# Modulation products queued behind named VectorE instructions, and gate scaling on ScalarE, in a one-core prefix network

## The chip, the cores and the metric

The kernel runs on one core of one Trainium2 chip. The metric is the device time of one execution in microseconds (us), given as the median of several runs.

## The reference, cut to what matters

A prefix network of two layers works on 256 latent tokens and 256 context tokens (together T = 512) of width 1024. Layer 0 is a hybrid mixer (HGRN2 scans in both directions over four heads of 128, and attention over eight heads of 64) and a convolutional FFN; layer 1 is an SSD mixer and an FFN. Both norms of every layer are modulated by vectors that come from the condition, one set for the latent and one for the context stream:

```python
for l in range(DEPTH):
    sh_m, sc_m, g_m, sh_f, sc_f, g_f = jnp.split(s_lat @ w_mod[l] + b_mod[l], 6, axis=-1)
    csh_m, csc_m, cg_m, csh_f, csc_f, cg_f = jnp.split(s_ctx @ w_mod[l] + b_mod[l], 6, axis=-1)
    u = modulate(h, norm_mix[l], sh_m, sc_m)       # rms_norm(h) * (1 + sc) + sh
    ...
    h = h + g_m[:, None] * y
    h = h + g_f[:, None] * conv_ffn(modulate(h, norm_ffn[l], sh_f, sc_f), ...)
```

The HGRN forget gates are `lb + (1 - lb) * sigmoid(f)`, and the keys `(1 - lb) * sigmoid(-f)`. The product of the condition with `w_mod` does not depend on the tokens, so it can be made at any time before its chunk (0 to 5, in the order of the split) is used.

## The kernel before

Activations are kept as fp32 split into a high and a low part (xhi, xlo; mhi, mlo; hh, hl). A weight tile of 128x1024 is loaded as `raw`, rounded by ScalarE into `whi` (L135) and the rest taken by VectorE into `wlo` (L137), and each product is three TensorE matmuls (L144): xlo by whi, xhi by whi, xhi by wlo. A step of 512 columns is about 0.23 us. Four buffers each hold raw, whi and wlo.

Layer 0's mixer goes: the first norm, with seven projections made along with it (L735 to L743); two HGRN pairs (`hgrn_pair`, two heads each); attention (`attention`: value projection L637, then `heads` and `mix` for four pairs of heads); the output projection (L774 to L782); then the FFN's norm and the FFN. In `hgrn_pair` a ladder of eight levels (L524 to L577) runs: at each level small matmuls of K by Q, then VectorE multiplications of Q, K and the running products f (L520). Then come K by Q in 128x128 (L584), four scalings for each head (`scl`, L589), transposes of K (L602), the states (L608), attention by v (L615), the states by Q (L619), and for each head y = ps * gain * gate (L625), its sum of squares by a matmul with ones (L628) and the scaled y (L630). Projections of the next stage are what TensorE does between these small matmuls. In `mix` each of the 32 softmax rows of tiles is: scores on TensorE, a bias for the latent stream (L691), a maximum (L693), the exponential on ScalarE (L695), a reciprocal and a scaling (L697) on VectorE, transposes back on TensorE (L700), and after four of them the product with v (L706).

A part of the modulation is made on VectorE. A unit is one 128x1024 tile `wv` of w_mod, multiplied with the two condition rows and summed: two instructions on `junk` (L270), here called halves, each with a read of the accumulator. Eight units make one chunk of modT (L276). At most three units are loaded ahead (`vec_fetch`). 64 units are made in this way: chunks (layer 0) 3, 4 and 2 in the mixer, and five more (chunk 5 of layer 0, and 0, 1, 3, 4 of layer 1) in FFN 0.

The instructions' order on each engine comes from a scheduler that works through the program in priority order as operands come free; each engine then runs its list strictly in order. `vec(n)` (L259) makes n units, and `issue_after(self.last_mm.ins)` keeps a unit in the list behind the most recent projection matmul. It is called after projections (L491, L506, L638, L650) and, for what is left, before the output projection (L771); FFN 0 calls it too. `after(...)` holds an instruction behind given ones.

The gate scalings of HGRN are VectorE instructions (L501, L503), eight of each, and the diagonal 32x32 blocks of the HGRN matrix are copied by VectorE (L552), four for each pair.

## Time and profile before

| | us |
|---|---|
| runs of the kernel before | 1226.21, 1227.2, 1228.07 (median 1227.2) |
| the profiled execution | 1228.9, its span 1227.1 |
| TensorE busy | 1196.0 (97%), mean granted clock 0.998 |
| VectorE busy | 923.7 (75%) |
| ScalarE busy | 593.1 (48%) |

The program's stages in the span are: first norm and first seven projections to about 71 us; HGRN pair 0 with its ladder to 138; pair 1 with its ladder to 212; attention to 327; output projection to 356; the FFN's norm to 363; FFN 0 after that. A window view gives for each stretch the busy time of every engine; where TensorE's falls short of the stretch, or its granted clock short of 1.00, time was lost. The timeline gives the instruction that began late and, in brackets, how long its engine had been idle and what ended that.

### The profile page before, as it was taken

How to read it: one execution, taken by the hardware profiler on the slowest of the kernel's cores; microseconds unless marked ns; L12 is line 12 of the kernel's file. 1: busy time of each engine (PE TensorE's matmuls, PEld its weight loads, DVE VectorE, ACT ScalarE, POOL GpSimd, SP SyncE). 2: the span in 40 equal slices, each digit the busy share in tenths (PEclk: the TensorE clock that was granted, in tenths of full speed). 3: DMA queues.
4: the chain of work that ended last, by engine and by line, in shares of the span. 5: the costliest groups of instructions: out<-in, count | busy, mean ns of one | idle time of the engine just before them, and what ended most of it. 6: DMA issues, size and time to landing. Idle time of an engine off the chain costs nothing.

```text
span 1227.1 us, 19142 instructions
## 1 busy us (share of the span) xinstructions
PE 1196.0 (97%) x7519; PEld 979.6 (80%) x7519; DVE 923.7 (75%) x1596; ACT 593.1 (48%) x923; POOL 0.2 (0%) x4
## 2 busy tenths in 40 slices
PE   5999999999999999999999999999999999999998
PEld 3687787766678888888888887778778798999998
DVE  4799999688669999984344458598989786766665
ACT  4554545798545331333133336647363644645452
POOL 0000000000000000000000000000000000000000
PEclk9999999999999999999999999999999999999999
DMA  9852635413064677752332234444344244665663
GB/s 379 316 178 71 222 106 169 136 60 125 27 213 148 207 213 227 226 178 82 104 102 83 90 119 139 154 138 160 113 138 138 86 148 144 190 187 184 181 185 106
DMA packets 55097, 189.35 MB, mean 154 GB/s; under 512 B 7136, under 2 KB 10848, under 8 KB 53728
## 3 DMA queue, kind: packets, MB, share of 16 engines
q1 hardware_dynamic: 51984, 185.17, 47.1%
q10 hardware_dynamic: 3024, 2.97, 0.8%
q8 instruction: 59, 0.97, 0.3%
q14 instruction: 30, 0.25, 0.1%
HBM read 187.00 MB, written 1.11 MB: 153 GB/s over the span
## 4 chain that ended last, share of the span: by engine, by line
PE 82%; DVE 8%; issue 2%; ACT 2%; DMA 1%; ACTq 0%; DVEq 0%
PE a L144 49%; PE s L144 17%; PE b L706 1%; PE s L161 1%; PE s L162 1%; PE s L163 1%; DVE junk L270 1%; DVE Q L520 1%; PE b L972 1%; PE b L999 1%; PE b L1004 1%; DVE wlo L137 1%; DVE K L520 1%; PE b L700 1%; PE b L937 1%
## 5 line engine op out<-in xcount | busy, mean ns | idle before, releaser
L135 ACT CAST whi<-raw 128x1024 fp32r<-128x1024 f32 (+1 forms) x234 | 240.9, 1032 | 342.7 <-PE a L144 275.2
L137 DVE TENSOR_TENSOR wlo<-raw,whi 128x1024 fp32r<-128x1024 f32 (+1 forms) x234 | 280.4, 1199 | 101.5 <-ACT whi L135 99.9
L144 PE MATMUL a<-xhi,wlo 128*128 128x512 f32 (+1 forms) x740 | 268.7, 370 | 3.6 <-ACT va L640 1.9
L144 PE MATMUL a<-xhi,whi 128*128 128x512 f32 (+1 forms) x740 | 271.4, 367 | 0.0
L144 PE MATMUL a<-xlo,whi 128*128 128x512 f32 (+1 forms) x740 | 258.5, 367 | 3.0 <-DVE xlo L378 3.0
L144 PEld LDWEIGHTS a<-xhi,wlo 128*128 128x128 f32 x740 | 139.0, 188 | 31.1 <-issue 4.1
L144 PEld LDWEIGHTS a<-xlo,whi 128*128 128x128 f32 x740 | 137.4, 188 | 31.8 <-issue 4.6
L144 PEld LDWEIGHTS a<-xhi,whi 128*128 128x128 f32 x740 | 139.4, 188 | 25.5 <-issue 3.6
L270 DVE SCALAR_TENSOR_TENSOR junk<-wv,rows 128x1024 f32<-128x1024 f32 x128 | 156.3, 1221 | 1.9
L144 PE MATMUL s<-xhi,wlo 128*128 128x512 f32 (+1 forms) x376 | 128.5, 342 | 0.0
L144 PE MATMUL s<-xhi,whi 128*128 128x512 f32 (+1 forms) x376 | 128.2, 341 | 0.0
L144 PE MATMUL s<-xlo,whi 128*128 128x512 f32 (+1 forms) x376 | 121.6, 341 | 0.4 <-ACT pr L695 0.4
L144 PE MATMUL a<-hh,whi 128*128 128x256 f32 (+1 forms) x359 | 120.1, 335 | 0.0
L144 PE MATMUL a<-hh,wlo 128*128 128x256 f32 (+1 forms) x359 | 113.2, 335 | 0.0
L144 PE MATMUL a<-hl,whi 128*128 128x256 f32 (+1 forms) x359 | 112.6, 336 | 0.0
L391 DVE SCALAR_TENSOR_TENSOR h<-a,modT,h 128x256 f32<-128x256 f32 x90 | 40.8, 481 | 69.4 <-PE a L144 69.2
L144 PEld LDWEIGHTS s<-xhi,wlo 128*128 128x128 f32 x376 | 70.6, 188 | 9.5 <-issue 0.4
L144 PEld LDWEIGHTS s<-xhi,whi 128*128 128x128 f32 x376 | 70.5, 188 | 9.1
L144 PEld LDWEIGHTS s<-xlo,whi 128*128 128x128 f32 x376 | 69.2, 188 | 10.2 <-ACT pr L695 0.8
L144 PEld LDWEIGHTS a<-hh,whi 128*128 128x128 f32 x359 | 67.6, 188 | 7.8
L144 PEld LDWEIGHTS a<-hl,whi 128*128 128x128 f32 x359 | 65.7, 188 | 8.2 <-DVE hl L399 0.5
L144 PEld LDWEIGHTS a<-hh,wlo 128*128 128x128 f32 x359 | 65.9, 188 | 7.8
(340 smaller groups left out, 1794.1 us busy)
## 6 DMA issues: line engine op xcount, KB each, us to landing
raw<-in_wup SPq DMA_DIRECT2D x88, 512.0 KB, 4.1
wv<-in_wmodT SPq DMA_DIRECT2D x64, 512.0 KB, 4.4
raw<-in_win SPq DMA_DIRECT2D x41, 512.0 KB, 3.7
raw<-in_wdn SPq DMA_DIRECT2D x32, 448.0 KB, 3.3
raw<-in_wo SPq DMA_DIRECT2D x24, 512.0 KB, 3.6
wm<-in_wmod SPq DMA_DIRECT2D x8, 1024.0 KB, 11.0
wv<-in_wmod SPq DMA_DIRECT2D x16, 512.0 KB, 4.6
raw<-in_wdn SPq DMA_DIRECT2D x16, 512.0 KB, 3.6
```

Of the source, the lines that this page charges most:

```text
L135: nc.scalar.copy(hi, raw)
L137: nc.vector.tensor_tensor(out=lo, in0=raw, in1=hi.bitcast(F32), op=ALU.subtract)
L144: self.last_mm = self.nc.tensor.matmul(ps, w, x, start=(first and i == 0), stop=(last and i == 2))
L161: mm(ps, xhi[:, k, tok], wlo[:, kk, :], start=(k == 0), stop=False)
L162: mm(ps, xhi[:, k, tok], whi[:, kk, :], start=False, stop=False)
L163: mm(ps, xlo[:, k, tok], whi[:, kk, :], start=False, stop=(k == NK - 1))
L270: nc.vector.scalar_tensor_tensor(out=self.junk, in0=w, scalar=1.0, in1=self.rows[:, s], op0=ALU.mult, op1=ALU.mult, accum_out=self.dots[:, ...
L391: self.nc.vector.scalar_tensor_tensor(out=self.h[:, n, s * S:(s + 1) * S], in0=ps[:, off:off + S], scalar=self.mod(l, chunk, n, s), in1=se ...
L520: mul = lambda o, t: nc.vector.tensor_tensor(out=o, in0=o, in1=t, op=ALU.mult)
L700: nc.tensor.transpose(pt[:, b * P:(b + 1) * P], pr[:, b * P:(b + 1) * P], self.ident)
L706: nc.tensor.matmul(po[64 * e:64 * e + 64, :S], va[:, b, hd * 64:(hd + 1) * 64], pTs[e][:, b, :], start=(b == 0), stop=(b == nkey - 1))
L937: nc.tensor.transpose(pt[:, b * P:(b + 1) * P], dst[:, b * P:(b + 1) * P], self.ident)
```

## The change

- A unit is issued as two separate halves. `half(x)` issues the next one, held behind the instruction x, or behind nothing if none is named.
- The wait for the last projection matmul is gone. Four halves stand behind the last xlo of the first norm (after each of four projections of pair 0: the one projection that is not made with the norm); one behind the Q, K, f multiplications of each level of the HGRN ladder (eight in a pair), four behind the last `scl`, one behind the scaling of each softmax row of tiles with qt == 1 (16), and two after each of the output columns 1 to 4, behind the sum of squares (`self.summed`).
- The units left over before the output projection are no longer made there; FFN 0 makes the rest, its halves held behind nothing.
- The chunks of layer 0 are made in the order 2, 4, 3 in place of 3, 4, 2.
- The gate scalings become ScalarE activations (Identity with scale and bias; Copy with scale), and the diagonal copies ScalarE copies.

```diff
-            with self.tc.issue_after(self.last_mm.ins):
-                for s in STREAMS:
-                    nc.vector.scalar_tensor_tensor(out=self.junk, in0=w, scalar=1.0, in1=self.rows[:, s], op0=ALU.mult,
-                                                   op1=ALU.mult, accum_out=self.dots[:, k, s:s + 1])
-            self.vec_fetch()
...
+    def half(self, after=None):
+        if not self.half_done:
+            if not self.fetched:
+                return
+            w, l, c, k = self.half_done = self.fetched.pop(0)
...
+            s = 0
+        else:
+            (w, l, c, k), self.half_done, s = self.half_done, None, 1
+        with self.after((after,) if after else ()):
+            nc.vector.scalar_tensor_tensor(out=self.junk, in0=w, scalar=1.0, in1=self.rows[:, s], op0=ALU.mult,
+                                           op1=ALU.mult, accum_out=self.dots[:, k, s:s + 1])
+        if s == 0:
+            return
+        self.vec_fetch()
...
-                        self.vec_queue([(0, 3), (0, 4), (0, 2)])
+                        self.vec_queue([(0, 2), (0, 4), (0, 3)])
...
-                    self.vec()
+                    if pr == 0:
+                        for _ in range(4):
+                            self.half(self.low.ins)
...
-                    nc.vector.tensor_scalar(out=ff, in0=ff, scalar1=om[:, d, hd:hd + 1], scalar2=lb[:, d, hd:hd + 1],
-                                            op0=ALU.mult, op1=ALU.add)
-                    nc.vector.tensor_scalar(out=kk, in0=kk, scalar1=om[:, d, hd:hd + 1], scalar2=None, op0=ALU.mult)
+                    nc.scalar.activation(ff, ff, AF.Identity, scale=om[:, d, hd:hd + 1], bias=lb[:, d, hd:hd + 1])
+                    nc.scalar.activation(kk, kk, AF.Copy, scale=om[:, d, hd:hd + 1])
...
-                    nc.vector.tensor_copy(blocks(j, 32, j, 32), attc[j:j + 32].rearrange("p (a b) t -> p a b t", a=4))
+                    nc.scalar.copy(blocks(j, 32, j, 32), attc[j:j + 32].rearrange("p (a b) t -> p a b t", a=4))
...
             for a in range(2):
-                mul(one(a, m, 0), one(a, m, 1))
+                x = mul(one(a, m, 0), one(a, m, 1))
+            self.half(x.ins)
...
-            scl(K[:, 1, hh, P:2 * P], tf(0, 0))
+            x = scl(K[:, 1, hh, P:2 * P], tf(0, 0))
+        for _ in range(4):
+            self.half(x.ins)
...
-                        nc.vector.tensor_scalar(out=pr, in0=pr, scalar1=sm[:, 2:3], scalar2=None, op0=ALU.mult)
+                        x = nc.vector.tensor_scalar(out=pr, in0=pr, scalar1=sm[:, 2:3], scalar2=None, op0=ALU.mult)
+                        if qt == 1:
+                            self.half(x.ins)
...
-            self.vec(NK * 3)
...
                     self.residual(0, 2, n, ps, part, True)
+                if 0 < n < 5:
+                    self.half(self.summed.ins)
+                    self.half(self.summed.ins)
```

The calls `self.vec(2)`, `self.vec(3)` and `self.vec()` after the value projections and the head projections go too. Lines of the changed kernel are 8 to 14 further down from there on.

How the lists move is shown at three places. The first is VectorE in the first norm. `junk` is a half, `mrow`, `mres`, `modT` and `A` make a late piece of chunk 1's modulation, `nt` is the normed activation, and `xlo` its low part for the last tiles. Before:

```order
L201 TENSOR_REDUCE mres_456<-m_399 128x2x4
L464 TENSOR_TENSOR lbm<-lbo,lbx 128x8
L270 SCALAR_TENSOR_TENSOR junk,dots_660<-wv_625,rows 128x1024
L210 TENSOR_TENSOR modT<-mres_456,c_bmod 128x2x4
L465 RECIPROCAL lbm<-lbm 128x8
L213 SCALAR_TENSOR_TENSOR A<-modT,c_gains 128x4
L270 SCALAR_TENSOR_TENSOR junk,dots_660<-wv_625,rows 128x1024
L375 SCALAR_TENSOR_TENSOR nt_494<-h,A,fr_173 128x256 x2
L375 SCALAR_TENSOR_TENSOR nt_528<-h,A,fr_173 128x256
L378 SCALAR_TENSOR_TENSOR xlo<-nt_494,modT,xhi 128x256 x2
L378 SCALAR_TENSOR_TENSOR xlo<-nt_528,modT,xhi 128x256
L375 SCALAR_TENSOR_TENSOR nt_528<-h,A,fr_173 128x256
```

After the change:

```order
L201 TENSOR_REDUCE mres_456<-m_399 128x2x4
L210 TENSOR_TENSOR modT<-mres_456,c_bmod 128x2x4
L213 SCALAR_TENSOR_TENSOR A<-modT,c_gains 128x4
L385 SCALAR_TENSOR_TENSOR nt_494<-h,A,fr_173 128x256 x2
L385 SCALAR_TENSOR_TENSOR nt_528<-h,A,fr_173 128x256
L388 SCALAR_TENSOR_TENSOR xlo<-nt_494,modT,xhi 128x256 x2
L388 SCALAR_TENSOR_TENSOR xlo<-nt_528,modT,xhi 128x256
L385 SCALAR_TENSOR_TENSOR nt_528<-h,A,fr_173 128x256
L137 TENSOR_TENSOR wlo_633<-raw_630,whi_632 128x1024
L388 SCALAR_TENSOR_TENSOR xlo<-nt_528,modT,xhi 128x256
L278 SCALAR_TENSOR_TENSOR junk,dots_660<-wv_623,rows 128x1024 x2
L769 CAST masks<-mf 128x160
```

The halves that stood among and ahead of nt and xlo now stand behind the last xlo.

The second is TensorE at the end of HGRN pair 1 (K transposed, states b<-v,kT, b<-att,v, b<-Q,Sx, sums b<-sq,ones); L161 to L163 are matmuls of attention's value projection, and L144 (a<-xhi,wlo) the first head projection. Before:

```order
L619 MATMUL b_1996<-Q_1195,Sx_1973 128x256 x2
L161 MATMUL a_2034<-wlo_2131,xhi 128x512
L162 MATMUL a_2034<-whi_2130,xhi 128x512
L163 MATMUL a_2034<-whi_2130,xlo 128x512
L161 MATMUL a_2035<-wlo_2131,xhi 128x512
L628 MATMUL b_2007<-sq_2003,ones 128x512
L615 MATMUL b_2012<-att_1625,v_1198 128x256 x4
L619 MATMUL b_2012<-Q_1195,Sx_1973 128x256 x2
L162 MATMUL a_2035<-whi_2130,xhi 128x512
L163 MATMUL a_2035<-whi_2130,xlo 128x512
L161 MATMUL a_2036<-wlo_2131,xhi 128x512
L162 MATMUL a_2036<-whi_2130,xhi 128x512
```

After the change:

```order
L616 MATMUL b_1989<-c_ident,K_1217 128x128 x4
L629 MATMUL b_2000<-att_1604,v_1219 128x256 x2
L622 MATMUL b_1978<-v_1219,kT_1976 128x128 x4
L629 MATMUL b_2000<-att_1604,v_1219 128x256 x2
L633 MATMUL b_2000<-Q_1216,Sx_1977 128x256 x2
L642 MATMUL b_2011<-sq_2007,ones 128x512
L629 MATMUL b_2016<-att_1604,v_1219 128x256 x4
L633 MATMUL b_2016<-Q_1216,Sx_1977 128x256 x2
L642 MATMUL b_2026<-sq_2023,ones 128x512
L144 MATMUL a_2170<-xhi,wlo_2174 128x512
L144 MATMUL a_2170<-xhi,whi_2173 128x512
```

The value projection's matmuls that stood between the small ones now stand further ahead, among the ladder's levels, and none is left here.

The third is VectorE at the start of the output projection; `h` is the residual of one output column, `nacc` the running sum of squares, wlo the weight split of a later column, which TensorE needs for column 4 (s_3361 before, s_3366 after the change). Before:

```order
L399 TENSOR_TENSOR mlo<-b_3182,mhi 128x256
L391 SCALAR_TENSOR_TENSOR h<-a_3218,modT,h 128x256 x2
L391 SCALAR_TENSOR_TENSOR h<-a_3253,modT,h 128x256 x2
L391 SCALAR_TENSOR_TENSOR h<-a_3289,modT,h 128x256 x2
L137 TENSOR_TENSOR wlo_3358<-raw_3355,whi_3357 128x1024
L318 TENSOR_TENSOR nacc_3245<-nacc_3245,nsq_3280 128x512
L391 SCALAR_TENSOR_TENSOR h<-s_3325,modT,h 128x256 x2
L318 TENSOR_TENSOR nacc_3245<-nacc_3245,nsq_3316 128x512
L137 TENSOR_TENSOR wlo_3395<-raw_3392,whi_3394 128x1024
L318 TENSOR_TENSOR nacc_3245<-nacc_3245,nsq_3352 128x512
L137 TENSOR_TENSOR wlo_3431<-raw_3428,whi_3430 128x1024
L137 TENSOR_TENSOR wlo_3467<-raw_3464,whi_3466 128x1024
```

After the change:

```order
L401 SCALAR_TENSOR_TENSOR h<-a_3284,modT,h 128x256 x2
L401 SCALAR_TENSOR_TENSOR h<-s_3325,modT,h 128x256
L328 TENSOR_TENSOR nacc_3236<-nacc_3236,nsq_3271 128x512
L278 SCALAR_TENSOR_TENSOR junk,dots_2649<-wv_3017,rows 128x1024
L401 SCALAR_TENSOR_TENSOR h<-s_3325,modT,h 128x256
L278 SCALAR_TENSOR_TENSOR junk,dots_2649<-wv_3017,rows 128x1024
L328 TENSOR_TENSOR nacc_3236<-nacc_3236,nsq_3311 128x512
L278 SCALAR_TENSOR_TENSOR junk,dots_2649<-wv_3088,rows 128x1024
L328 TENSOR_TENSOR nacc_3236<-nacc_3236,nsq_3352 128x512
L278 SCALAR_TENSOR_TENSOR junk,dots_2649<-wv_3088,rows 128x1024
L137 TENSOR_TENSOR wlo_3363<-raw_3360,whi_3362 128x1024
L286 TENSOR_TENSOR modT<-dots_2649,c_bmod 128x16
```

Four halves now stand ahead of that wlo. Ten more follow up to the last `nacc` of the norm: four that are held behind `nacc`, and six that FFN 0's calls make.

## Rows read from the trace of the kernel before

**Rows 1.** The page: span, and busy time of each engine.
```profile
span 1227.1 us, 19142 instructions
...
PE 1196.0 (97%) x7519; PEld 979.6 (80%) x7519; DVE 923.7 (75%) x1596; ACT 593.1 (48%) x923; POOL 0.2 (0%) x4
```

**Rows 2.** Windows by stage: length, busy time of PE, PEld, DVE, ACT, POOL, clock, DMA.
```profile
71.00:122.00 51.00, 49.16 (x720) 40.83 (x718) 50.62 (x97) 26.47 (x44) 0.00 (x0) 1.00 0.37 124
...
138.00:205.00 67.00, 66.04 (x794) 54.10 (x793) 66.30 (x122) 29.56 (x46) 0.00 (x0) 1.00 0.48 151
205.00:212.00 7.00, 5.06 (x22) 3.51 (x21) 6.77 (x13) 4.58 (x9) 0.00 (x0) 1.00 0.57 166
...
363.00:600.00 237.00, 237.00 (x1017) 190.44 (x1017) 196.62 (x311) 79.67 (x102) 0.00 (x0) 1.00 0.59 183
```

**Rows 3.** Windows of line L270 (the halves) alone: length, DVE busy, clock, DMA.
```profile
219.00:363.00 144.00, 1.23 (x2) 1.00 0.31 98
363.00:545.00 182.00, 90.93 (x148) 1.00 0.67 209
```

**Rows 4.** Groups of DVE by form: count, busy us, mean ns, idle before.
```profile
L137 DVE TENSOR_TENSOR wlo<-raw,whi 128x1024 fp32r<-128x1024 f32 x194 | 236.8, 1222 | 78.6 <-ACT whi L135 77.0
L270 DVE SCALAR_TENSOR_TENSOR junk<-wv,rows 128x1024 f32<-128x1024 f32 x128 | 156.3, 1221 | 1.9
...
L552 DVE COPY att<-attc 32x256 f32<-32x256 f32 x8 | 2.3, 283 | 0.1
```

**Rows 5.** Timeline of DVE in the first norm: start, us, instruction.
```profile
53.18 1.22 DVE L270 SCALAR_TENSOR_TENSOR junk<-wv,rows 128x1024 f32<-128x1024 f32 x1
...
57.48 1.22 DVE L270 SCALAR_TENSOR_TENSOR junk<-wv,rows 128x1024 f32<-128x1024 f32 x1
...
59.81 1.27 DVE L378 SCALAR_TENSOR_TENSOR xlo<-nt,modT,xhi 128x256 fp32r<-128x256 f32 x3
```

**Rows 6.** Timeline of PE in the first norm; in brackets idle before and releaser.
```profile
59.05 0.40 PE L144 MATMUL b<-xhi,wlo 128*128 128x512 f32 x1
60.74 0.50 PE L144 MATMUL a<-xlo,whi 128*128 128x512 f32 x1 [1.30 <-DVE xlo L378]
```

**Rows 7.** Waits of PE: us in total, times, longest.
```profile
PE a L144 <- ACT va L640: 1.9, 1, 1.9
...
PE b L542 <- DVE Q L520: 1.0, 1, 1.0
...
PE m L199 <- DVE mrow L193: 0.9, 1, 0.9
```

**Rows 8.** Timeline of DVE in pair 1: last ladder scaling, first y.
```profile
195.56 0.47 DVE L589 TENSOR_SCALAR K<-K,f 128x128 f32<-128x128 f32 x2
...
203.30 0.75 DVE L625 SCALAR_TENSOR_TENSOR h<-b,c_small,h 128x512 f32<-128x512 f32 x1
```

**Rows 9.** Timeline of PE in pair 1: first level, end of the tail, head projection.
```profile
166.25 0.76 PE L542 MATMUL b<-h,kc 128*32 128x32 f32 x64
...
208.21 0.80 PE L163 MATMUL a<-whi,xlo 128*128 128x512 f32 x1
...
209.31 0.39 PE L163 MATMUL s<-whi,xlo 128*128 128x512 f32 x1
211.64 0.50 PE L144 MATMUL a<-xhi,wlo 128*128 128x512 f32 x1 [1.94 <-ACT va L640]
```

**Rows 10.** Windows: softmax part of attention, output, the slowed stretch, its gap; a dense part.
```profile
239.25:323.60 84.35, 82.73 (x409) 56.20 (x407) 67.81 (x158) 71.20 (x162) 0.00 (x0) 1.00 0.24 77
327.42:358.13 30.71, 30.70 (x174) 25.49 (x177) 19.78 (x33) 14.66 (x19) 0.00 (x0) 1.00 0.40 123
212.30:215.70 3.40, 3.40 (x10) 2.62 (x9) 3.33 (x5) 2.03 (x3) 0.00 (x0) 0.51 0.91 266
...
266.00:303.00 37.00, 36.14 (x173) 24.06 (x171) 32.84 (x71) 34.22 (x74) 0.00 (x0) 1.00 0.32 109
```

**Rows 11.** Timeline of ACT before pair 1, and a window of ACT alone there.
```profile
138.78 1.28 ACT L499 ACT_TABLE_LOAD   x1
140.07 0.60 ACT L499 ACTIVATE f<-a 128x512 f32<-128x512 f32 x1
...
131.30:166.20 34.90, 16.85 (x24) 1.00 0.63 196
```

More of the change, by code (lines that the diff above doesn't have):

```diff
@@ L259, in vec @@
     def vec(self, n=1):
+        for _ in range(2 * n):
+            self.half()
+    def half(self, after=None):
         nc = self.nc
-        for _ in range(n):
+        if not self.half_done:
             if not self.fetched:
                 return
-            w, l, c, k = self.fetched.pop(0)
+            w, l, c, k = self.half_done = self.fetched.pop(0)
             if k == 0:
                 self.dots = self.w.tile([P, NK, 2], F32, tag="dots", bufs=2, name=self.nm("dots"))
-            with self.tc.issue_after(self.last_mm.ins):
-                for s in STREAMS:
-                    nc.vector.scalar_tensor_tensor(out=self.junk, in0=w, scalar=1.0, in1=self.rows[:, s], op0=ALU.mult,
-                                                   op1=ALU.mult, accum_out=self.dots[:, k, s:s + 1])
-            self.vec_fetch()
-            if k < NK - 1:
-                continue
-            dst = self.modT[:, l, 8 * c:8 * c + 8, :]
-            nc.vector.tensor_tensor(out=dst, in0=self.dots, op=ALU.add,
-                                    in1=cust(self.bmod[:, l, 8 * c:8 * c + 1], 0, [[1, 8], [0, 2]]))
-            if c in (1, 4):
-                which = (c - 1) // 3
-                nc.vector.scalar_tensor_tensor(
-                    out=self.A[:, l, which], in0=dst, scalar=1.0, op0=ALU.add, op1=ALU.mult,
-                    in1=cust(self.gains[:, 2 * which + l, 0:1], 0, [[1, NK], [0, 2]]))
@@ L284, in mod @@
+        nc.vector.tensor_tensor(out=dst, in0=self.dots, op=ALU.add,
+                                in1=cust(self.bmod[:, l, 8 * c:8 * c + 1], 0, [[1, 8], [0, 2]]))
+        if c in (1, 4):
+            which = (c - 1) // 3
+            nc.vector.scalar_tensor_tensor(
+                out=self.A[:, l, which], in0=dst, scalar=1.0, op0=ALU.add, op1=ALU.mult,
+                in1=cust(self.gains[:, 2 * which + l, 0:1], 0, [[1, NK], [0, 2]]))
     def mod(self, l, chunk, k, s):
@@ L317, in sumsq @@
             self.act_set(6, last)
-        nc.vector.tensor_tensor(out=self.acc[:, tok], in0=self.acc[:, tok], in1=sq, op=ALU.add)
+        self.summed = nc.vector.tensor_tensor(out=self.acc[:, tok], in0=self.acc[:, tok], in1=sq, op=ALU.add)
     def norm_r(self, ps, t0, n, meanwhile):
@@ L377, in norm_u @@
             u = nc.scalar.activation(xhi[:, k, tok], t[:, rel], AF.Identity, bias=sh)
-            nc.vector.scalar_tensor_tensor(out=xlo[:, k, tok], in0=t[:, rel], scalar=sh, in1=xhi[:, k, tok].bitcast(F32),
-                                           op0=ALU.add, op1=ALU.subtract)
+            self.low = nc.vector.scalar_tensor_tensor(out=xlo[:, k, tok], in0=t[:, rel], scalar=sh, op0=ALU.add,
+                                                      in1=xhi[:, k, tok].bitcast(F32), op1=ALU.subtract)
         return u
@@ L545, in hgrn_pair @@
                     for a in range(2):
-                        nc.vector.tensor_tensor(out=flat(Q, a), in0=q.rearrange("p h t -> p (h t)"), in1=flat(f, a),
-                                                op=ALU.mult)
+                        x = nc.vector.tensor_tensor(out=flat(Q, a), in0=q.rearrange("p h t -> p (h t)"), in1=flat(f, a),
+                                                    op=ALU.mult)
+                    self.half(x.ins)
                     continue
@@ L696, in mix @@
                         nc.vector.reciprocal(sm[:, 2:3], sm[:, 1:2])
-                        nc.vector.tensor_scalar(out=pr, in0=pr, scalar1=sm[:, 2:3], scalar2=None, op0=ALU.mult)
+                        x = nc.vector.tensor_scalar(out=pr, in0=pr, scalar1=sm[:, 2:3], scalar2=None, op0=ALU.mult)
+                        if qt == 1:
+                            self.half(x.ins)
                         pt = self.ps_b()[:, :w]
```

7 lines of the change are left out of this document (3 added, 4 removed).

## The prediction

> **What bounds the kernel now.** I read the page first: TensorE is busy for 1196.0 of 1227.1 us, VectorE for 75%, ScalarE for 48% [rows 1]. So a change to VectorE's list can win only what TensorE loses now, about 31 us in all, and only the part of it that lies in the first 363 us, where the halves are moved. The window view by stage shows how little that is [rows 2]: TensorE idles for 1.84 us of 71 to 122, for 0.96 of 138 to 205, for 1.94 of 205 to 212, and for nothing in FFN 0. In the same rows VectorE is full in HGRN (50.62 of 51, 66.30 of 67), so the halves there do stand in TensorE's way a little. The windows of the halves' line show the other side [rows 3]: between 219 and 363 us there is one half, and 74 of the 128 lie in FFN 0, where TensorE is never short. The change carries 20 halves out of HGRN, where VectorE is full, and ten out of FFN 0, and puts them into attention (16) and the output projection (14), where there are none. What counts is whether those two stages have room on VectorE.
>
> **Price of a half.** 1221 ns, and a wlo 1222 ns [rows 4]; with overlaps a step is 1.15 to 1.2 us, and I take 1.2.
>
> **First norm: -2.2.** Four halves sit among nt and xlo [rows 5], and TensorE, which had started a matmul of 0.23 us at 59.05, gets its next xlo at 60.74, a gap of 1.46 us that ends at VectorE's xlo [rows 6]. The wait of 0.9 on mrow [rows 7] has a half ahead of mrow as well. The lists show the halves behind the last xlo, so both go, about 1.4 and 0.8. The next thing that could be late is the weight split, which the matmuls need anyway; I leave a tenth or two for it.
>
> **Ladder of pair 0: -0.8 (0 to -1.9).** TensorE's idle time here is 1.84 us, 1.0 of it one wait for Q [rows 2, 7]. The lists give the ladder 24.0 us of projection matmuls for cover where they gave it 17.5, and VectorE eight halves for what were two, less the copies (8 take 2.3 us, so 1.2 in a pair [rows 4]). Chain and cover grow by about the same; I take half of the idle time as gained.
>
> **Pair 1: +3.8 (-4.6 to +5.5).** Before, the first level begins at 166.25 and the first head projection at 211.64, 45.4 later [rows 9]; the last ladder scaling ends at 196.0, 29.8 after the level [rows 8]. There is no half in that ladder now. Seven are put ahead of the last scaling (7 x 1.2 = 8.4), and four copies (1.2) and one wlo (1.2) leave: 35.8. In VectorE's list four halves and three wlo follow, 8.4 more, before the first y: 44.2. From the first y (203.30) to the start of the last value matmuls at 208.21, behind the second sum of squares, it is 4.9 us [rows 8, 9]: 49.1, or 3.7 to 3.9 later than now. TensorE cannot use that time: the value projection, whose matmuls stand between the small ones of this tail now, is spent among the levels, so the tail is bare. What is won is in there already: the wait of 1.94 us between 209.31 and 211.64, behind ScalarE's copies of va [rows 7, 9], goes, because the copies run during the tail. The low end is all idle time of 138 to 212 closed (0.96 + 1.94) and no slowed stretch (1.7); the high end is a second one. **The clock:** behind the gap the granted clock is 0.51 for 3.4 us [rows 10], that is the lower level, 1.2 GHz; it costs half of that, 1.7 us. I expect the same after the bare tail, so no difference.
>
> **Scaling and copies on ScalarE: 0 (0 to +3).** 16 scalings and 8 copies leave VectorE. ScalarE gets, ahead of pair 1, eight scalings of at most 0.6 each (the price of the sigmoid on the same shape) and four more table loads of 1.28 [rows 11], as its list has Ln, Exp and sigmoid in turn at the border of the pairs: 4.8 + 5.1 on top of 16.85 us in a stretch of 34.9 [rows 11], 26.8. It is covered by the projections of pair 1; without that cover pair 1 would begin late. The Trainium skill, page "ScalarE: Activation LUTs", section "What ACT_TABLE_LOAD costs", adds a drain of about 1380 ns to each switch of tables. By that price the estimate for the same stretch would be 32.3 of 34.9 us, and hardly any slack would be left. The trace does not show the drain: the sigmoid starts at 140.07, 1.29 after the load did [rows 11].
>
> **Attention: +6 (+2.7 to +15.6).** From the first maximum to the last scaling it is 84.35 us, with VectorE busy for 67.81 and TensorE for 82.73 [rows 10]. Sixteen halves add 19.2: VectorE's 87.0 alone exceed the stretch by 2.7, which is the low end; TensorE gets 2.3 us of output projection into it, 85.1, a little under that. VectorE waits for scores, for ScalarE's exponential and for the head norms, and not all of these waits can be filled, since a half that has begun delays the maximum behind it by up to 1.2. In the dense part, 266 to 303, VectorE is busy for 32.84 of 37, 89% [rows 10]; at 87% the stretch would take 100, the high end. In HGRN, the one stage where halves stand among the steps that TensorE waits for, VectorE reached 99% [rows 2], which would be 87.9. I take 96%, nearer to HGRN because it is the same arrangement: 90.5, or +6.
>
> **Output projection: +6.5 (+6.0 to +8).** From the end of the last product with v (327.42) to the start of the norm's rsv (358.13) it is 30.71 us, in which VectorE is busy for 19.78 [rows 10]. 14 halves stand between the same two instructions now, 16.8 us: 36.6, so VectorE becomes the bound by 5.9 even if it never waited; the first residuals wait for their matmuls a little, and overlaps give some back. TensorE, which needs 28.4 after the part that moved into attention, waits about 6 us for the wlo behind four halves. That these ten halves of FFN 0 are gone later is worth nothing, since FFN 0 is TensorE's alone (237.00 of 237 [rows 2]).
>
> **Norm of the FFN: -0.4,** as its mrow transposes are moved into FFN 0 and the wait on them goes. Everything behind is unchanged.
>
> **Sum.** -2.2 - 0.8 + 3.8 + 0 + 6 + 6.5 - 0.4 = +12.9. The profiled execution took 1228.9, so it would take 1241.8; it lies 1.7 over the median of the runs shown, 1227.2, from which the sum gives 1240.1. I forecast **1240**.
>
> **The rivals.** Each is the forecast with one term exchanged, on the median's basis.
> - *Not slower: the waits close and attention takes its halves for nearly nothing.* If VectorE's lighter list closes the idle time of both pairs (1.84 + 0.96 + 1.94) and the clock stays up (1.7), with the first norm's 2.2 and the norm's 0.4 that is -9.0; attention at VectorE's floor is +2.7 and the output +6.0. That gives -0.3, 1227; busy times overlap a little at each instruction, and if the 174 there (158 and the halves [rows 10]) overlap by 0.015 us or more each, it is below 1224.7. It decides where attention's stretch stays under 87.1 us and the first head projection starts without a wait. For it: VectorE was full in both pairs. Against it: the bare tail in TensorE's list. 0.18.
> - *Only the output loses.* Pair 1 comes out even, because the first y does not wait for the three wlo and the four halves as summed, and attention is at its floor: -2.2 - 0.8 + 0 + 2.7 + 6.5 - 0.4 = +5.8, 1233. 0.22.
> - *Attention keeps its waits.* +15.6 in place of +6: 1249.7. The dense part speaks for it, HGRN against it. 0.12.
> - *The clock falls more often.* In the bare tail TensorE has some 9 us of work in about 17, and before the late wlo it stands for 6. A second and third stretch like that of rows 10 cost 1.7 each: 1242 to 1243.5. The Trainium skill, page "TensorE: Matmul & The Clock Gate", section "Loop structure matters more than you think", says that the loop nest decides whether matmuls stay at the full clock, and long waits between them lose it. The trace agrees for the wait of 1.94 us, and shows that the shorter gaps of the ladders leave the clock at 1.00 [rows 2]. 0.08.
> - *ScalarE late for pair 1.* Its slack of 34.9 - 26.8 turns out to be gone because the table loads stand between a sigmoid and its scaling; two loads late is +2.6, 1242.7. The drain that the Trainium skill gives ("ScalarE: Activation LUTs", "What ACT_TABLE_LOAD costs") would speak for it. 0.04.
> - *The change does not do what it says.* In one point it does not: six halves of FFN 0 run in the output stage though nothing there calls them. That is in the sum; were they late in place of there, the output term would be 7.2 less.
>
> **How the numbers follow.** The forecast has 0.36. A difference of 0.2%, 2.5 us, is about what a measurement of this kernel can tell from none. Faster than 1224.7 needs the first rival with more overlap than counted, two thirds of its chance: 0.11. Within 0.2%: the rest of it and the low edge of the second, 0.11. Slower: 0.78. The range takes in the second rival, the forecast with its bounds, and most of the third: 1227 to 1249.
>
> **What the profile of the changed kernel would show.** The first norm without the gap of 1.46 us at xlo. In pair 1 no matmul of the value projection in the tail, TensorE idle for several microseconds there, and the first head projection 48 to 50 us after the first level. In attention VectorE over 93% busy, and the stretch from the first maximum to the last scaling at about 90 us. In the output a wait of TensorE for wlo of 4 to 7 us, and 36 to 38 us from the last product with v to rsv. FFN 0 with the same length. The prediction is wrong if attention's stretch stays under 87 us, if TensorE runs through the output without that wait, or if the tail of pair 1 is no longer than now.

## The result, and the profile after

The changed kernel takes 1253.68 us (median of 4 runs, 1251.97 to 1255.22), the kernel before beside it 1226.79: a ratio of 1.0214, with a 95% interval of 1.0202 to 1.0227. It is slower by 2.1%, in the direction that was forecast and by twice the size; 1240 was said, with a range up to 1249. The profiled execution took 1254.38, against 1228.9 before, and its span is 25.5 us longer.

The page of the changed kernel, span and busy time; the lines answer to [rows 1]:

```profile
span 1252.6 us, 19123 instructions
...
PE 1205.6 (96%) x7519; PEld 984.4 (79%) x7519; DVE 913.8 (73%) x1572; ACT 610.4 (49%) x950; POOL 0.2 (0%) x4
```

VectorE has less to do than before (913.8 for 923.7), as the scalings and copies left it. TensorE has the same 7519 matmuls and is busy 9.6 us longer with them: most of that is the clock. In the stretches at the lower clock shown below it is busy for 19.1 us, in the trace of before for 3.4 [rows 10]; half of the difference, 7.9 us, is what the clock can account for, and the remaining 1.7 is not followed here. Its idle time grew by 15.9.

The windows of the changed kernel by stage, with the columns of [rows 2] and [rows 10]. The fourth is from the first maximum to the last scaling of attention, the fifth from the last product with v to the norm's rsv, the last FFN 0:

```profile
71.00:122.00 51.00, 50.48 (x720) 41.95 (x719) 44.77 (x82) 31.46 (x53) 0.00 (x0) 1.00 0.33 105
138.00:205.00 67.00, 64.62 (x786) 52.59 (x785) 53.56 (x94) 39.09 (x61) 0.00 (x0) 1.00 0.33 104
205.00:212.00 7.00, 3.53 (x13) 2.12 (x12) 2.25 (x4) 3.82 (x7) 0.00 (x0) 0.94 0.41 152
239.02:338.52 99.50, 89.35 (x419) 60.27 (x417) 84.23 (x191) 72.68 (x163) 0.00 (x0) 0.97 0.31 102
342.41:382.26 39.85, 32.41 (x167) 25.47 (x167) 35.80 (x60) 14.58 (x19) 0.00 (x0) 0.87 0.53 174
387.00:624.00 237.00, 237.00 (x1024) 190.31 (x1017) 192.52 (x303) 78.91 (x103) 0.00 (x0) 1.00 0.58 179
```

Attention takes 99.50 in place of 84.35, the output stage 39.85 in place of 30.6, and FFN 0 is as full as it was. Set side by side by the first and last instruction of each part, with the terms of the prediction (the last product with v ends at 327.49 in the trace of before; the 327.42 of [rows 10] is the start of the matmul behind it):

| part, from ... to ... | before | after | difference | forecast |
|---|---|---|---|---|
| start to the first ladder level of pair 0 | 87.95 | 85.69 | -2.3 | -2.2 |
| to the first level of pair 1 | 78.30 | 76.55 | -1.7 | -0.8 |
| to the first head projection | 45.39 | 49.44 | +4.1 | +3.8 |
| to the first maximum | 27.61 | 27.34 | -0.3 | 0 |
| to the last scaling | 84.35 | 99.50 | +15.1 | +6 |
| to the end of the last product with v | 3.88 | 3.88 | 0.0 | 0 |
| to the norm's rsv | 30.64 | 39.86 | +9.2 | +6.5 |
| to the end of the span | 869.0 | 870.3 | +1.3 | -0.4 |

The parts up to the scores are nearly as forecast. Two parts hold the rest: attention and the output. The last 1.3 us has 1.7 of clock in it: the trace has a stretch at the lower clock at 1061 us, in layer 1, which the trace of before has not.

**Pair 1** came out at the forecast length, but not wholly by the forecast way. Windows from the first level to the end of the last scaling, and from there to the first head projection, before:

```profile
166.25:196.03 29.78, 28.82 (x579) 22.32 (x578) 29.49 (x65) 12.96 (x22) 0.00 (x0) 1.00 0.24 79
196.03:211.64 15.61, 13.67 (x69) 10.33 (x67) 15.24 (x26) 8.35 (x13) 0.00 (x0) 1.00 0.66 198
```

and after:

```profile
162.24:196.47 34.23, 33.21 (x596) 25.61 (x596) 33.08 (x70) 15.67 (x27) 0.00 (x0) 1.00 0.28 83
196.47:211.68 15.21, 10.38 (x51) 7.19 (x50) 10.78 (x15) 7.51 (x12) 0.00 (x0) 0.98 0.56 200
```

The ladder, where VectorE is full, is 4.4 us longer, and the tail is no longer than before. TensorE has as little idle time in the ladder as before (1.0 us) and stands idle in the tail for 4.8 us in place of 1.9, because the projections were used up in the ladder. Timeline of TensorE (first level, second sum of squares, first head projection), as [rows 9]:

```profile
162.24 0.76 PE L552 MATMUL b<-h,kc 128*32 128x32 f32 x64
...
207.77 1.12 PE L642 MATMUL b<-sq,ones 128*128 128x512 f32 x2 [0.69 <-ACT sq L636]
211.68 0.79 PE L144 MATMUL a<-xhi,wlo 128*128 128x512 f32 x1 [2.78 <-ACT va L653]
```

and of VectorE (last half, first y), as [rows 8]:

```profile
203.22 1.22 DVE L278 SCALAR_TENSOR_TENSOR junk<-wv,rows 128x1024 f32<-128x1024 f32 x1
...
204.37 0.75 DVE L639 SCALAR_TENSOR_TENSOR h<-b,c_small,h 128x512 f32<-128x512 f32 x1
```

The first y begins 42.1 us after the first level, 2.1 earlier than summed. The wait for va, which was to go, is there and longer, 2.78 in place of 1.94: ScalarE's list has the copies behind the square roots of the tail, and behind the last of these it stands for 0.76 us more, until VectorE's scaled y. The two misses cancel.

**Attention.** TensorE's waits from the first maximum to the last scaling, total, times, longest:

```profile
PE s L698 <- ACT pr L707: 7.0, 5, 2.2
PE b L714 <- DVE pr L709: 1.5, 3, 1.1
PE a L144 <- DVE xlo L409: 0.8, 1, 0.8
```

Scores wait for ScalarE's exponential to free their place, and transposes for VectorE's scaling. One such wait, on TensorE, and on ScalarE and VectorE around it:

```profile
279.24 0.39 PE L144 MATMUL a<-xhi,wlo 128*128 128x512 f32 x1
281.87 0.50 PE L698 MATMUL s<-kl,qs 128*128 128x512 f32 x1 [2.25 <-ACT pr L707]
```

```profile
279.73 1.24 ACT L683 CAST kl<-kl 64x512 fp32r<-64x512 f32 x2
280.88 0.36 ACT L715 COPY pT<-b 128x256 f32<-128x256 f32 x1
281.26 0.47 ACT L707 ACTIVATE pr<-s,sm 128x256 f32<-128x256 f32 x1
...
281.72 0.68 ACT L707 ACTIVATE pr<-s,sm 128x512 f32<-128x512 f32 x1
```

```profile
282.05 0.35 DVE L709 TENSOR_SCALAR pr<-pr,sm 128x256 f32<-128x256 f32 x1
282.32 1.22 DVE L278 SCALAR_TENSOR_TENSOR junk<-wv,rows 128x1024 f32<-128x1024 f32 x1
283.46 0.08 DVE L278 DVE_READ_ACCUMULATOR junk<-wv,rows 128x1 f32 x1
283.46 0.16 DVE L708 RECIPROCAL sm<-sm 128x1 f32<-128x1 f32 x1
```

The exponential at 281.26 comes behind casts of the next heads' keys in ScalarE's list; the reciprocal of the next tile, whose exponential is done by 282.4, begins at 283.46, behind the half. Steps of one chain (scores, maximum, exponential, reciprocal, scaling, transposes) stand behind work that is not in it. In this wait, the longest, that work is ScalarE's, and no half stands directly ahead of it.

The 15.1 us split by the windows: TensorE's idle time goes from 1.62 (84.35 less 82.73 [rows 10]) to 10.15, +8.5; 2.3 us of output projection (ten matmuls more) are moved in; its busy time is longer by 4.3 beyond that. Of these, 3.4 are the clock, two stretches of 3.4 us at the lower level, 1.2 GHz; the other 0.9 is not followed. The stretches at the lower clock in this trace, the first behind the wait for va, the second and third in attention, the fourth in the output, the last in layer 1:

```profile
211.10:214.51 3.41, 2.83 (x7) 2.25 (x8) 0.00 (x0) 3.28 (x5) 0.00 (x0) 0.50 0.40 115
282.78:286.19 3.41, 3.41 (x11) 1.33 (x9) 2.16 (x6) 1.57 (x4) 0.00 (x0) 0.50 0.48 139
320.32:323.74 3.42, 3.42 (x16) 2.28 (x16) 3.29 (x9) 1.70 (x5) 0.00 (x0) 0.50 0.40 138
351.04:361.28 10.24, 6.05 (x14) 4.79 (x15) 9.92 (x15) 0.63 (x1) 0.00 (x0) 0.50 0.72 224
1061.01:1064.43 3.42, 3.42 (x19) 3.42 (x18) 3.28 (x9) 1.61 (x5) 0.00 (x0) 0.50 0.34 127
```

**Output.** TensorE, before and behind its long wait, and VectorE at its end:

```profile
349.30 0.28 PE L144 MATMUL a<-xhi,whi 128*128 128x256 f32 x1
355.23 0.80 PE L144 MATMUL s<-xhi,wlo 128*128 128x512 f32 x1 [5.66 <-DVE wlo L137]
```

```profile
352.82 1.22 DVE L278 SCALAR_TENSOR_TENSOR junk<-wv,rows 128x1024 f32<-128x1024 f32 x1
353.96 0.08 DVE L278 DVE_READ_ACCUMULATOR junk<-wv,rows 128x1 f32 x1
353.96 1.22 DVE L137 TENSOR_TENSOR wlo<-raw,whi 128x1024 fp32r<-128x1024 f32 x1
```

TensorE waits 5.66 us for the wlo behind the fourth half, as the lists said, and then works at half its clock. Of the 9.2 us, its idle time is +7.4 (39.85 less 32.41, against 0.01 before), the work moved into attention -2.3, and the remaining 4.1 is its longer busy time: 3.0 of that is the clock (6.05 us of work at the lower level), the other 1.1 is not followed.

### The profile page after: what moved, and what is told of

It reads as the page before. It is cut to its first block, busy times and chain, and to the rows that moved or that the text cites. A ratio compares the mean times of both kernels' runs of the same rounds, so it can differ in the third digit from the quotient of the medians.

```text
span 1252.6 us, 19123 instructions
## 1 busy us (share of the span) xinstructions
PE 1205.6 (96%) x7519; PEld 984.4 (79%) x7519; DVE 913.8 (73%) x1572; ACT 610.4 (49%) x950; POOL 0.2 (0%) x4
## 4 chain that ended last, share of the span: by engine, by line
PE 85%; DVE 7%; ACT 5%; DMA 2%; issue 1%; SPq 0%; ACTq 0%; DVEq 0%
PE a L144 49%; PE s L144 17%; PE b L720 1%; PE s L162 1%; PE s L163 1%; PE s L161 1%; PE b L1015 1%; PE b L988 1%; PE b L1020 1%; DVE junk L278 1%; DVE Q L530 1%; PE b L953 1%; ACT whi L135 1%; PE b L144 1%; DVE wlo L137 1%
## 5 line engine op out<-in xcount | busy, mean ns | idle before, releaser
L144 PE MATMUL a<-xhi,wlo 128*128 128x512 f32 (+1 forms) x740 | 268.8, 370 | 4.6 <-ACT va L653 2.8
L144 PE MATMUL a<-xhi,whi 128*128 128x512 f32 (+1 forms) x740 | 271.5, 367 | 0.0
L144 PE MATMUL a<-xlo,whi 128*128 128x512 f32 (+1 forms) x740 | 258.1, 367 | 2.6 <-ACT whi L135 1.0
L144 PEld LDWEIGHTS a<-xhi,wlo 128*128 128x128 f32 x740 | 139.1, 188 | 32.6 <-issue 3.8
L144 PEld LDWEIGHTS a<-xlo,whi 128*128 128x128 f32 x740 | 138.1, 189 | 32.5 <-issue 4.4
L144 PEld LDWEIGHTS a<-xhi,whi 128*128 128x128 f32 x740 | 139.6, 189 | 25.4 <-issue 3.5
L144 PE MATMUL s<-xhi,wlo 128*128 128x512 f32 (+1 forms) x376 | 129.7, 345 | 5.7 <-DVE wlo L137 5.7
L144 PE MATMUL s<-xhi,whi 128*128 128x512 f32 (+1 forms) x376 | 129.3, 344 | 0.0
L144 PE MATMUL s<-xlo,whi 128*128 128x512 f32 (+1 forms) x376 | 122.9, 344 | 0.0
L144 PE MATMUL a<-hh,whi 128*128 128x256 f32 (+1 forms) x359 | 120.1, 335 | 0.0
L144 PE MATMUL a<-hh,wlo 128*128 128x256 f32 (+1 forms) x359 | 113.1, 335 | 0.0
L144 PE MATMUL a<-hl,whi 128*128 128x256 f32 (+1 forms) x359 | 112.5, 336 | 0.0
L144 PEld LDWEIGHTS s<-xhi,wlo 128*128 128x128 f32 x376 | 71.4, 190 | 15.1 <-DVE wlo L137 5.9
L144 PEld LDWEIGHTS s<-xhi,whi 128*128 128x128 f32 x376 | 71.4, 190 | 9.3
L144 PEld LDWEIGHTS s<-xlo,whi 128*128 128x128 f32 x376 | 70.0, 190 | 9.1
L144 PEld LDWEIGHTS a<-hh,whi 128*128 128x128 f32 x359 | 67.5, 188 | 7.7
L144 PEld LDWEIGHTS a<-hl,whi 128*128 128x128 f32 x359 | 65.7, 188 | 8.2 <-DVE hl L409 0.5
L144 PEld LDWEIGHTS a<-hh,wlo 128*128 128x128 f32 x359 | 66.0, 188 | 7.8
```

Source lines behind the costliest of these rows:

```text
L144: self.last_mm = self.nc.tensor.matmul(ps, w, x, start=(first and i == 0), stop=(last and i == 2))
```

## The experiments

The first theory (A): the 16 halves of attention make its loss, the 14 of the output make VectorE the bound there, and HGRN's part is even.

**1. No halves in attention.**

```diff
-                        if qt == 1:
-                            self.half(x.ins)
...
-                        self.vec_queue([(0, 2), (0, 4), (0, 3)])
+                        self.vec_queue([(0, 2), (0, 4)])
```

> The changed kernel without the 16 halves in attention: they are left out, and chunk 3 of layer 0 (a shift) is set to zero instead, so 16 halves of the 128 are not made. Everything else is as changed; 10 halves stand in the output projection in place of 14. Theory A (the 16 halves are what costs in attention, in VectorE's list and by TensorE's lower clock behind the waits): the stretch from the first maximum to the last scaling falls from 99.4 to 84 to 87 us, the output stretch from 39.9 to about 35, and the time is 1231 to 1236 us. Rival B (attention was slowed by what comes before it, the bare tail of pair 1 and ScalarE's other order, and not by its halves): the stretch stays over 93 us and the time over 1242.

Measured: 1239.44 us, ratio 1.0098 (1.0083 to 1.0113). Attention is back to before: window from the first maximum to the last scaling, and the halves' line alone in the output stage (a half counts two, with its read of the accumulator):

```profile
237.61:321.99 84.38, 82.76 (x409) 56.22 (x407) 67.81 (x158) 71.23 (x162) 0.00 (x0) 1.00 0.22 77
```

```profile
325.87:365.38 39.51, 17.18 (x28) 0.91 0.54 184
```

Rival B falls: the bare tail and all of HGRN are as changed here, and attention takes 84.38. The time missed its window because the output did not shrink: 14 halves stood there again, not 10, since FFN 0's calls filled the places that came free, and the stretch stayed at 39.5. So the output's loss does not hang on attention's.

**2. The output relieved.**

```diff
-                if 0 < n < 5:
+                if 3 < n < 6:
                     self.half(self.summed.ins)
                     self.half(self.summed.ins)
...
-            self.vec_queue([(0, 5), (1, 0), (1, 1), (1, 3), (1, 4)])
...
             self.norm_mod(l, 1, xhi, xlo, streams, p)
+            if not last:
+                self.vec_queue([(0, 5), (1, 0), (1, 1), (1, 3), (1, 4)])
```

> The changed kernel with the output projection relieved: only the four halves that chunk 3 still needs stand there, behind columns 4 and 5, and chunk 5's units are fetched and made behind the FFN's norm. All 128 halves are made. Theory A (VectorE's 14 halves are the bound of the output stage): from the last product with v to the norm's first instruction 31 to 33 us in place of 39.9, no wait of TensorE for wlo, and the time 1244 to 1248 us. Rival C (the output stage is late because of what attention leaves, and of the clock): the stretch stays over 36 us and the time over 1250.

Measured: 1242.44 us, ratio 1.0125 (1.011 to 1.0141), 11.2 less than the changed kernel. The stretch is 30.29:

```profile
341.56:371.85 30.29, 29.18 (x163) 23.39 (x167) 24.72 (x42) 14.58 (x19) 0.00 (x0) 1.00 0.50 162
```

Rival C falls. Theory A stands so far, though more was won than it gave.

**3. Four halves ahead of the wlo.** As run 2, with the same number of halves at the place where the change has its first four: `if 0 < n < 3`.

> The changed kernel with four halves in the output projection in place of 14: the same four that stand ahead of the wlo which TensorE needs for column 4, behind columns 1 and 2. Chunk 5's units are fetched and made behind the FFN's norm, as in the run with the output relieved, which had its four behind columns 4 and 5 and took 30.7 us from the last product with v to the norm's first instruction. Theory A (the sum of VectorE's work is the bound there): 24.6 us of work, so again 30.5 to 32 us, and 1241 to 1244 us in all. Rival F (what costs is the one late wlo: TensorE waits for it, and its clock falls behind the wait): 35 to 39 us, and 1246 to 1251.

Measured: 1251.52 us, ratio 1.0196 (1.0174 to 1.0218). The stretch and TensorE's longest wait in it:

```profile
341.50:380.17 38.67, 31.91 (x164) 25.31 (x167) 24.53 (x42) 14.58 (x19) 0.00 (x0) 0.87 0.38 126
```

```profile
PE s L144 <- DVE wlo L137: 5.7, 1, 5.7
```

This decides it for rival F. VectorE is busy for 24.7 and 24.5 us in the two runs, TensorE has the same matmuls, and the stretch is 30.3 with the four halves behind the wlo and 38.7 with them ahead of it. Theory A's part on the output is wrong: not the sum of VectorE's work but one late operand and the clock behind it cost 8.4 of the 9.2 us over the kernel before. The other ten halves of the changed kernel cost 1.2.

**4. The change in the first norm and HGRN alone.** The halves of attention and output are taken out, `self.vec(3)`, `self.vec()` and `self.vec(NK * 3)` put back where the kernel before has them, and halves without a named instruction are held behind the last matmul again.

> The change in the first norm and in HGRN alone (halves behind the last xlo, the ladder levels and the last scaling; gate scaling and diagonal copies on ScalarE); the rest of chunks 2, 4 and 3 is made where the kernel before makes units, behind the value and head projections. Theory A (HGRN's part is even: 2.2 and 1.7 won, 4 lost in the bare tail of pair 1, and nothing else): 1225 to 1230 us. Rival D (the order of HGRN also spoils attention): 1233 or more.

Measured: 1237.86 us, ratio 1.0091 (1.0075 to 1.0108). A miss: +10.4 where about 0 was expected, and a time that rival D gave. The first two parts are won (-3.2 and -1.7), 4.1 are lost in pair 1, and attention takes 92.06. But this is not HGRN's doing at a distance: the units that HGRN no longer made were made in attention, 9 halves of them, as the halves' line in that window shows:

```profile
240.06:332.12 92.06, 11.04 (x18) 0.96 0.31 105
```

**5. The same, with chunk 5's units later** (the last two parts of the diff of run 2), which leaves three halves in attention.

> The run with the HGRN part only, with chunk 5's units fetched and made behind the FFN's norm; three halves stand in attention's list in place of six and more, and the order of the other engines there differs a little. Theory G: the stretch from the first maximum to the last scaling is 84.4 + 3 x 1.2 = 88, and the time 1231 to 1235 us. Rival D (what HGRN leaves behind, the bare tail and the other order, spoils attention, and not the halves): 91 us or more, 1236 and over.

Measured: 1234.31 us, ratio 1.0055 (1.0037 to 1.0072), and 87.35 for attention, 3.0 for three halves. Rival D falls. What then remains over the kernel before is mostly pair 1 (+4.1) and 5.2 from the first score to the last product with v, 3.0 of them in the stretch named.

**6. The 16 halves in eight pairs.**

```diff
-                        if qt == 1:
+                        if qt == 1 and e == 1:
                             self.half(x.ins)
+                            self.half(x.ins)
```

> The changed kernel with its 16 attention halves in eight pairs, each behind the last scaling ahead of a product with v, where VectorE's longest waits (for mhi) lie, in place of one behind each scaling with qt == 1. Theory G (a half costs its whole length in attention wherever it stands, since scores, maximum, exponential, scaling and transposes are one chain through VectorE's list): the stretch from the first maximum to the last scaling stays at 96 to 101 us. Rival H (only the place is wrong; VectorE's waits of 17 us could take the halves): 86 to 92 us, and 1240 to 1246 us in all.

Measured: 1248.77 us, ratio 1.017 (1.0153 to 1.0186); attention 92.14:

```profile
239.13:331.27 92.14, 85.49 (x406) 57.21 (x405) 82.91 (x189) 71.72 (x162) 0.00 (x0) 0.98 0.35 110
```

Just outside rival H's stretch: 7.8 of the 15.1 us remain. Without the 2.3 us of output projection that the changed kernel moved in and this one does not, the loss falls from 12.8 to 7.8. The same halves cost 0.80 us each behind every second scaling and 0.49 in pairs ahead of the products, with one stretch of low clock in place of two. The whole time is over what H gave, as the output was untouched (38.7).

**7. Short halves in attention.** The 16 halves there are cut to 256 columns.

```diff
-            nc.vector.scalar_tensor_tensor(out=self.junk, in0=w, scalar=1.0, in1=self.rows[:, s], op0=ALU.mult,
+            nc.vector.scalar_tensor_tensor(out=self.junk[:, :n], in0=w[:, :n], scalar=1.0, in1=self.rows[:, s, :n], op0=ALU.mult,
...
-                            self.half(x.ins)
+                            self.half(x.ins, 256)
```

> The changed kernel with the 16 halves in attention cut to a quarter of their columns (256 of 1024; three quarters of these products are left out). Their number and calls stay. Theory G (the length of a half is what delays the chain of scores, maximum, exponential, scaling): a half is then 0.35 to 0.45 us in place of 1.2, and the stretch from the first maximum to the last scaling falls to 86 to 91 us. Rival (it is the order that more instructions force on the other engines, whatever their length): 95 to 100 us.

Measured: 1240.17 us, ratio 1.0111 (1.0097 to 1.0125). The group of the short halves (their mean is 417 ns), and the window of attention:

```profile
L278 DVE SCALAR_TENSOR_TENSOR junk<-wv,rows 128x256 f32<-128x256 f32 x16 | 6.7, 417 | 0.0
```

```profile
239.99:324.52 84.53, 82.09 (x410) 56.49 (x408) 72.68 (x191) 71.42 (x162) 0.00 (x0) 1.00 0.37 120
```

16 of them cost 0.2 us in all, less than expected. So the number alone costs nothing. The cost is far from proportional to the length: halves of 0.42 us cost next to nothing, halves of 1.22 do. No stretch of low clock is left in attention either. What stays open is how much of the loss is the half itself and how much the order that the scheduler makes of the other engines' lists for it: ScalarE's list in attention is another one here than in the changed kernel, and so it is in runs 1 and 6. No pair of these runs has the same lists and different halves.

**8. The kernel before with two parts of the change:** units of pair 0 behind the last xlo, scaling and copies on ScalarE.

> The kernel before with two parts of the change: the units of pair 0 are queued behind the last xlo of the first norm, and gate scaling and diagonal copies run on ScalarE. Its tail of pair 1 keeps the value projection between the small matmuls. Theory A: the first norm's 2.2 us are won and the waits at the end of HGRN shrink: 1221 to 1225 us. Rival E (ScalarE with four more table loads is late for pair 1 and gives it back): 1226 to 1230.

Measured: 1226.09 us, ratio 0.999 (0.9981 to 1.0): unclear, nearer to rival E. The first two parts win 3.0 and 1.1, but from there the first head projection takes 1.2 us longer and waits 3.3 for va, and the way from it to the first maximum takes 1.1 longer, with the lower clock for 6.8 us there. Pair 1 does not begin late, so the time is rival E's and its reason is not.

**9. The same with chunk 5's units later.**

> The kernel before with the units of pair 0 behind the last xlo of the first norm, gate scaling and copies on ScalarE, and chunk 5's units fetched and made behind the FFN's norm, so that six halves leave the border of HGRN and attention. Theory A: the 1.2 us that the run without the last part lost ahead of the first head projection come back: 1222 to 1225 us. Rival: they do not, since the wait there is ScalarE's: 1225.5 to 1227.

Measured: 1225.2 us, ratio 0.9978 (0.9969 to 0.9988): a little faster, between the two ranges. The wait for va was still 2.8, so what came back is not what the expectation named.

**10. Only the first norm, chunk 5 later;** scaling and copies on VectorE.

> The kernel before with only the units of pair 0 behind the last xlo and chunk 5's units behind the FFN's norm; scaling and copies stay on VectorE. Against the run that has these two and the scaling on ScalarE (1225.2): if the scaling on ScalarE is worth its 9 us of VectorE (VectorE is the one that is full in HGRN), 1226 to 1229; if it is worth nothing, 1224.5 to 1225.7.

Measured: 1223.42 us, ratio 0.9976 (0.9966 to 0.9987). Below both ranges, and no worse than run 9 with the scaling on ScalarE, so the 9 us that it takes off VectorE are worth nothing measurable. The traces even speak against it: from the first level of pair 1 to the first head projection run 9 takes 46.1 us and run 10 takes 44.9, with a wait for va of 1.6 in place of 2.8.

**11. Only chunk 5 later.**

> The kernel before with only chunk 5's units fetched and made behind the FFN's norm, so that six halves leave the end of HGRN. If the wait of 1.9 us ahead of the first head projection and the slowed stretch behind it hang on these halves: 1223 to 1225.5. If they hang on ScalarE's copies alone: 1226.5 to 1228.5.

Measured: 1226.78 us, ratio 1.0 (0.9992 to 1.0009). Nothing by itself: the wait for va is 1.9, as before. With run 10, the first norm's placement carries the gain.

**12. First norm and pair 0 as changed, the rest as before, chunk 5 later.** In run 5's kernel the halves of the ladder are issued only `if pr == 0`, and pair 1 has `self.vec()` behind its projections and `self.vec(2)` behind its values. The four halves behind the last scaling were left in both pairs, so it is not pair 0 alone as the expectation says.

> The change in the first norm and in pair 0 alone (four halves behind the last xlo, one behind each ladder level, four behind the last scaling, scaling and copies on ScalarE); pair 1, attention and output make units as before, and chunk 5's are fetched and made behind the FFN's norm. All 128 halves are made, 48 of them ahead of attention and none in attention or output. Theory A: pair 0 wins about 4 us to the first level of pair 1 as in all runs of the changed kernel, the tail of pair 1 keeps its projections, attention stays at 84.4 and output at 31: 1221 to 1224.5 us. Rival: VectorE, with the 20 halves of pair 1 and after, gives back the win ahead of the scores: 1225 to 1228.

Measured: 1223.38 us, ratio 0.9972 (0.9961 to 0.9984): faster than both kernels, and no faster than run 10. Windows of pair 1 as above, first head projection, and the windows behind it and of attention:

```profile
162.02:192.29 30.27, 28.06 (x576) 21.91 (x576) 30.07 (x62) 14.61 (x26) 0.00 (x0) 1.00 0.33 101
192.29:208.21 15.92, 14.30 (x71) 10.81 (x69) 15.38 (x24) 8.46 (x13) 0.00 (x0) 1.00 0.54 183
```

```profile
208.21 0.51 PE L144 MATMUL a<-xhi,wlo 128*128 128x512 f32 x1 [1.62 <-ACT va L662]
```

```profile
208.00:214.00 6.00, 5.79 (x25) 4.69 (x26) 4.15 (x8) 3.02 (x6) 0.00 (x0) 1.00 0.87 264
234.28:318.69 84.41, 82.84 (x409) 56.20 (x407) 67.75 (x158) 71.26 (x162) 0.00 (x0) 1.00 0.23 77
```

To the first level of pair 1 it is 162.02, 4.2 less than before; 46.2 from there to the head projection, for its ladder is 30.3 long and its tail has projections between the small matmuls; and there is no slowed stretch behind it. The tail has more halves than that of the changed kernel (five ahead of the first y, there four), so halves behind the last scaling alone do not make the loss.

## Why the prediction was right and wrong

- **First norm, -2.2:** right, -2.3, though not by its terms. TensorE's waits for xlo up to 71 us fall from 2.6 to 0.3 in all, where 1.4 was counted, and the wait for mrow, which was to go with 0.8, is still 0.5. That the sum came out is partly luck.
- **Ladder of pair 0, -0.8:** right in kind, -1.7, near the low end of its bounds. The trace of before has four halves between the first level and the last scaling, not the two of the sum; run 10 has four there too, and has -1.2 of the gain.
- **Pair 1, +3.8:** right in size, +4.1, in every run that has halves on this ladder's levels and the bare tail behind it (49.4 us in runs 1 to 7). Run 12 has neither and takes 46.2, so the two together cost 3.2; no run has one of them alone. The other 0.8 is about what pair 1 loses with the scaling on ScalarE (runs 9 and 10). Two points were wrong and cancel: the first y came 2.1 us earlier than summed, and the wait for va did not go.
- **Scaling on ScalarE, 0:** right as far as the times tell; runs 9 and 10 show no gain, and in their traces pair 1 is 1.2 us longer with it, inside the 0 to +3. Pair 1 did not begin late (162.24 for 166.25), so the drain that the Trainium skill gives for each table load ("ScalarE: Activation LUTs", "What ACT_TABLE_LOAD costs") cost nothing here.
- **Attention, +6:** this step failed, and it holds most of the miss: +15.1. The failing sentence is the choice of 96% "because it is the same arrangement" as in HGRN. VectorE reached 85% (84.23 of 99.50). What the runs showed in its place: TensorE's idle time there grew by 8.5 us, 7.0 of its waits are for ScalarE's exponential, and the clock took 3.4 more; without the halves (run 1) or with short ones (run 7) the stretch is 84.4 and 84.5. That each tile goes back and forth between three engines, while in HGRN VectorE's own chain is the longest, is the likely reason; it is argued and not shown. The nearest row was the dense part of attention itself, 89% [rows 10], which the prediction read and set aside; by it the stretch is 97.8, or +13.4. The upper bound of +15.6, from 87%, is close to what came, partly by luck, since it has neither the clock nor the work moved in.
- **Output, +6.5:** the wait for wlo was named and came (about 6 forecast, 5.66 measured), but the term was worked out from the sum of VectorE's work, and that was not the bound: run 3 takes 38.7 us with ten halves fewer. This step failed as well. The cost was the wait of 5.7 plus the clock behind it, 3.0, which the sum left out because VectorE was to be the bound.
- **The clock:** the rival that it falls more often was right (0.08), at 3.4 us in attention, which it did not name, and 3.0 in the output, where 1.7 to 3.4 was said in all. It came together with the rival that attention keeps its waits (1249.7, 0.12). Waits of TensorE stand ahead of both, and they should have been weighed together; taking them as separate cases made the range end too low. That 1249.7 and the clock's 3.4 make 1253, about what was measured, is partly luck, for the +15.1 of attention has 3.4 of clock in it already. The Trainium skill's rule ("TensorE: Matmul & The Clock Gate", "Loop structure matters more than you think") that long waits between matmuls lose the full clock agrees with the trace: 0.50 behind the wait for wlo. Run 1 shows that it is not each long wait that does so: 1.00 behind 2.78 us.
- **Norm, -0.4:** not seen. From rsv to FFN 0 it is 4.98 for 4.66, with a new wait of 1.9 us for the DMA of wv, and the rest of the span is 1 us longer, with the stretch at the lower clock at 1061 in it.

## What to carry to other kernels

Filler work on an engine has a price by its place: ask how long one piece of it is beside the slack of the chain that passes through that engine's list, not whether the engine is idle a fifth of the time. Pieces of 0.4 us vanished in attention, while 16 pieces of 1.2 us lengthened it by 15.1, 2.3 of that work moved in. Look above all for the one operand that the bottleneck needs next and that now stands behind filler, and price its wait with a stretch at half the clock behind it, as most of the long waits had here. And take what the measurement shows to be good out of a bundle: the first norm's placement was worth 3.4 us (runs 10 and 11), and the rest of the change hid it.

## What was not expected of the hardware

The granted clock fell behind most of TensorE's long waits, but the length of the wait does not tell by itself. In the changed kernel it was at the lower level, 1.2 GHz, behind 2.78 us of idling ahead of the first head projection, in the kernel before behind 1.94 [rows 10], and in attention behind 2.25 and 1.41. It stayed at 1.00 at the same place behind 1.62 us in run 12, and behind the same 2.78 us in run 1:

```profile
211.54 0.50 PE L145 MATMUL a<-xhi,wlo 128*128 128x512 f32 x1 [2.78 <-ACT va L654]
```

```profile
211.54:215.00 3.46, 3.46 (x15) 2.83 (x16) 0.00 (x0) 2.69 (x4) 0.00 (x0) 1.00 0.38 114
```

A wait of 1.28 us in layer 1 has the lower clock behind it in the changed kernel (at 1061) and the full clock in the kernel before. And in run 3 the clock fell where TensorE had not been idle at all for 14 us:

```profile
800.00:814.00 14.00, 14.00 (x84) 1.00 0.44 134
814.04:817.46 3.42, 3.42 (x9) 0.50 0.49 162
```

What decides it, no run here shows. What such a stretch costs, the traces do show: from the first head projection to the first score it is 25.6 us in runs 1 and 12, which kept the clock, 27.2 in the kernel before and 26.9 in the changed one. In the output the lower clock lasted longer, and 6.05 us of work done at it behind a single wait cost 3.0.
